# Weight sums of w_down made in DRAM ahead of the down projection, and its products in a new order

## The chip, the cores and the metric

The kernel runs on one core of a Trainium2 chip, and the other cores are idle. The metric is the device time of one execution in microseconds (us). Kernels are compared by the median of several executions; a comparison is called faster or slower from 2% on.

## What is computed

One layer of a bidirectional encoder, all in float32, on 512 tokens of width 1024 with 256 memory tokens:

```
n = rms_norm(x);  proj = n @ w_in                       # 1024 x 4608
ya = s5_branch(proj[:, :512])                           # state-space scan both ways, GLU
yb = sgu_branch(zu, zv)                                 # gated mixing in chunks of 128 tokens
h = x + (sigmoid(ga) * (ya @ w_proj_a) + sigmoid(gb) * (yb @ w_proj_b)) @ w_out
h = h + cross_attention(rms_norm(h), rms_norm(mem))     # w_q, w_k, w_v, w_xo; 4 heads
h = h + (silu(hn @ w_gate) * (hn @ w_up)) @ w_down      # w_down: 2816 x 1024
out = rms_norm(h)
```

The change concerns the last product, with w_down: 512 tokens by 2816 by 1024.

## The kernel before, in words

Every matrix product runs in a two-part float32r form: each operand is split into a high and a low part (`split`, lines 83 to 86: a cast on ScalarE and a subtraction on VectorE), and three TensorE matmuls, high by high, high by low and low by high, make one product (`mm3`). So each weight block is loaded, split, and used.

The stages follow each other: the norm of x and its transposition; half of `zv`; the S5 input; the other half of `zv`; the gates `ga`; `zu`; the gates `gb` with w_proj_b; the GLU and w_proj_a; w_out; w_k, w_v, w_q with the attention; w_xo; the gate and up units; the down projection. The S5 scan is a generator (`s5_program`) whose pieces are worked off beside the matmuls of the other mixers, by a credit that `tick` hands out.

**The weight plan.** All weight blocks stand in one list, `plan`, in the order of their use. Each entry has a key, a list of loads with a lead (how many blocks before its use the load is issued), and a function that makes the split operands. `next_w` (line 287) is called for each block: it calls `begin` for the entries up to FAR blocks ahead, which issues every load whose lead is due, and splits the blocks up to SPLITS = 2 ahead. An ordinary block is 512 KB, has a lead of LOADS = 3, lands in one of three `raw` buffers by a transfer on SyncE's queue (SP), and is split into one of three pairs of `hi` and `lo` buffers.

**The order on the engines.** The source issues through a tile framework with `schedule_with_timeline_sim=True`: at compile time a scheduler puts the instructions of each engine and queue in order, by the source's order and by when it expects their operands and buffers to be there, and it adds all semaphore waits. The position in the source is therefore not by itself the position in a queue. On the chip each engine and each queue then keeps its order. SP issues plain transfers, ScalarE's queue (ACT) a few more; GpSimd (POOL) issues transfers that add to their destination, and also computes the `pow` of the norms, clears the buffers `bd` and `ss` of the S5 part, adds in the merge and moves the S5 kernels through DRAM (`kd`, `tt`).

**Seven products.** The gate, up and down projections use a scheme with seven half-size products in place of eight: numbers 1 to 7, each of a sum of token quarters by a sum of weight quarters, with results added and subtracted. In the units (`plan_unit`) the weight sums are made by an adding transfer and by VectorE. In the down projection (`plan_down`, line 206) the quarter of w_down is 1408 by 512. It is cut into CHUNKS = 6 pieces (five of 2 x 128 rows, 512 KB, and one of 128 rows, 256 KB); one product is 66 matmuls with 512 columns, over two token tiles. Before the change the weight operands come like this:

- product 1: the first quarter, loaded into six tiles (`grown`) of the units' buffers, five blocks ahead;
- products 5, 6 and 4: the same tiles, after each use grown by another quarter with an adding transfer on POOL's queue (`grow`, line 222), which can start only when the split of that piece is done;
- products 2 and 3: plain loads into the `raw` buffers;
- product 7: a plain load into a large tile (`third_start`, line 231), and an adding transfer onto it (`third_add`, line 234), 16 and 14 blocks ahead.

The token operands are made by `make_tokens` (line 1326): for each product three pieces are split, and with products 5, 6 and 2 VectorE makes the next token sums in place. The results go onto `h` with `onto_h`; `first_half` and `finish` are the two halves of the last norm. The order of products is DOWN = 1, 5, 6, 2, 7, 3, 4, written out by hand a second time in the calls of `down_product` at the end.

Of the kernel before, what the change touches and what calls it, by code (L numbers as in the profile page):

```python
# [9 lines left out]
F32 = mybir.dt.float32  # L10
F32R = mybir.dt.float32r
AF = mybir.ActivationFunctionType
ALU = mybir.AluOpType
# [4 lines left out]
P = 128  # L18
D = 1024
T = 512  # L20
NT = T // P
KD = D // P
# [11 lines left out]
NF = FF // P  # L34
# [18 lines left out]
def hybrid_layer_kernel(  # L53
# [8 lines left out]
    nc = tc.nc  # L62
# [3 lines left out]
    w_gate, w_up, w_down = w_gate[0], w_up[0], w_down[0]  # L66

    cp = ctx.enter_context(tc.tile_pool(name="const", bufs=1))
    wp = ctx.enter_context(tc.tile_pool(name="weights", bufs=3))
    sp = ctx.enter_context(tc.tile_pool(name="slots", bufs=1))  # L70
    np_ = ctx.enter_context(tc.tile_pool(name="norm", bufs=2))
    dp = ctx.enter_context(tc.tile_pool(name="scratch", bufs=1, space=DRAM))
# [10 lines left out]
    def split(dst_hi, dst_lo, src, lo_eng=None):  # L83

        nc.scalar.copy(dst_hi, src)  # L85
        (lo_eng or nc.vector).tensor_tensor(dst_lo, src, dst_hi.bitcast(F32), ALU.subtract)  # L86
# [1 line left out]

    LOADS, SPLITS, FAR = 3, 2, 16
    plan, tiles = [], []

    def block(w, kb, k, c0, n):
        return w[kb * P:(kb + k) * P, c0:c0 + n].rearrange("(k p) c -> p k c", p=P)

    def halves(src, j=None, place=None):
        _, k, n = src.shape
        if place is None:
            hi = wp.tile([P, k, n], F32R, tag="hi", name="whi", bufs=3)  # L100
            lo = wp.tile([P, k, n], F32R, tag="lo", name="wlo", bufs=3)
        else:
            hl = sums_place(place, k, n)
            hi, lo = hl[:, 0], hl[:, 1]
        split(hi, lo, src, nc.gpsimd if j is not None and j < 2 else None)
        return hi, lo
# [3 lines left out]
    def sums_place(i, k, n, shift=0):  # L110
        t = sums_pool[0].tile([P, 2 * k * n + 128], F32R, tag=f"s{i}", name=f"s{i}", bufs=1)
        return t[:, shift:shift + 2 * k * n].rearrange("p (h k n) -> p h k n", h=2, k=k)
# [20 lines left out]
    def plan_feat(w, c0, nk, kpt=4):  # L133
        for kb in range(0, nk, kpt):
            plan_block(w, kb, kpt, c0, 256)

    def plan_tok(w, c0, nk, kpt=2):
        for kb in range(0, nk, kpt):
            plan_block(w, kb, kpt, c0, 512)
# [7 lines left out]
    stp = [None]  # L147
# [52 lines left out]

    DOWN, CHUNKS = (1, 5, 6, 2, 7, 3, 4), 6
    third = []

    def plan_down(w, make_tokens):
        def b(i, jc, c):
            row, k = (4 * c + 2 * i, 2) if c < CHUNKS - 1 else (NF - 2 + i, 1)
            return block(w, row, k, 512 * (1 - jc), 512)

        grown, got = {}, {}

        def view(t, c):
            return t if c < CHUNKS - 1 else t[:, 0:1]

        def first(c):
            nm = ("t", "b22", "b21")[c % 3]
            grown[c] = stp[0].tile([P, 2, 512], F32, tag=nm, name="grown", bufs=2)
            nc.sync.dma_start(view(grown[c], c), b(0, 0, c))

        def grow(c, src):
            nc.gpsimd.dma_start(view(grown[c], c), src, accum_op=ALU.add)

        def plain(q, c, src):
            got[q, c] = wp.tile([P, 2, 512], F32, tag="raw", name="wraw", bufs=3)
            nc.sync.dma_start(view(got[q, c], c), src)

        def third_start(c):
            if not third:
                third.append(token_place("t3", F32).rearrange("p (c k n) -> p c k n", c=8, k=2))  # L230
            nc.sync.dma_start(view(third[0][:, c], c), b(0, 1, c))

        def third_add(c):
            nc.gpsimd.dma_start(view(third[0][:, c], c), b(1, 1, c), accum_op=ALU.add)

        for q in DOWN:
            for c in range(CHUNKS):
                loads = {1: [(5, lambda c=c: first(c))],
                         2: [(LOADS, lambda c=c: plain(2, c, b(1, 0, c)))],
                         3: [(LOADS, lambda c=c: plain(3, c, b(1, 1, c)))],  # L240
                         7: [(16, lambda c=c: third_start(c)), (14, lambda c=c: third_add(c))]}.get(q, [])

                def make(q=q, c=c):
                    if c % 2 == 0:
                        make_tokens(q, c // 2)
                    src = got.pop((q, c)) if q in (2, 3) else third[0][:, c] if q == 7 else grown[c]
                    ops_ = halves(view(src, c))
                    if q in (1, 5, 6):
                        grow(c, b(*{1: (0, 1), 5: (1, 1), 6: (1, 0)}[q], c))
                    return ops_  # L250

                plan.append(((w, q, c), loads, make))

    plan_tok(w_in, OFF_V, KD)
    for c0 in range(0, SW, 256):
        plan_feat(w_in, c0, KD)
    plan_tok(w_in, OFF_V + 512, KD)
    for c0 in range(0, D, 256):
        plan_feat(w_in, OFF_GA + c0, KD)
    for c0 in range(0, GW, 256):  # L260
# [20 lines left out]
    UNITS = [(w, c0) for c0 in range(0, FS, 512) for w in (w_gate, w_up)]  # L281
    plan_units(UNITS)
    down_tokens = []
    plan_down(w_down, lambda q, c: down_tokens[0](q, c))
    used_w = [0]

# [192 lines left out]
    def slot(tag, shape, dt, name):  # L479
        return sp.tile(list(shape), dt, tag=tag, name=name)  # L480

    def token_place(name, dt, shift=0):
        t = sp.tile([P, 2 * KD * T + 128], dt, tag="B", name=name)
        return t[:, shift:shift + 2 * KD * T]

    def token_slot(name, shift=0):

        hl = token_place(name, F32R, shift).rearrange("p (h k t) -> p h k t", h=2, k=KD)
        return hl[:, 0], hl[:, 1]


# [557 lines left out]
    h = slot("A", (P, NT, D), F32, "h")  # L1049
# [45 lines left out]
    shift = ap_.tile([P, 16], F32, name="shift")  # L1095
# [87 lines left out]
    fn = (fn_hi, fn_lo)  # L1183
# [89 lines left out]
    def unit_bank(name):  # L1273
        return bank(name).rearrange("p (j t) -> p j t", j=2)
# [7 lines left out]
    def put(u, f, ts, src):  # L1282
        dst = acts(u[1] // 512, f)[:, :, ts]
        if u[0] is w_gate:
            nc.scalar.activation(dst, src, AF.Silu)
        else:
            nc.vector.tensor_tensor(dst, dst, src, ALU.mult)
# [38 lines left out]
    def make_tokens(q, c):  # L1326
        hl = sums_place((1, 2, 4)[len(made) % 3], 4, 256)
        made[q, c] = (hl[:, 0], hl[:, 1])
        f, ts = {1: (0, T0), 5: (0, T1), 6: (0, T1), 2: (1, T0), 7: (0, T0), 3: (1, T0), 4: (1, T1)}[q]
        for src, ks in token_pieces(f, ts, c):  # L1330
            split(hl[:, 0, ks], hl[:, 1, ks], src)
        a, b_, c_, d_ = (token_pieces(f_, ts_, c) for ts_ in (T0, T1) for f_ in (0, 1))
        for (q11, _), (q12, _), (s21, _), (q22, _) in zip(a, b_, c_, d_):
            if q == 5:
                V.tensor_tensor(s21, s21, q11, ALU.subtract)
            elif q == 6:
                V.scalar_tensor_tensor(q11, s21, -1.0, q22, ALU.mult, ALU.subtract)
            elif q == 2:
                V.tensor_tensor(q12, q12, s21, ALU.add)
# [3 lines left out]
    for i, u in enumerate(UNITS):  # L1343
        final = i == len(UNITS) - 1
        x, v = begun
        q = unit_bank("pq")
# [38 lines left out]
    def first_half(t, half):  # L1385

        early[t] = half
        sum_sq(hss[:, 2, t, half:half + 1], h[:, t, HALF[half]])
        nc.vector.tensor_tensor(hg[:, t, :], h[:, t, HALF[half]], g_o[:, HALF[half]], ALU.mult)
        nc.vector.tensor_scalar(msq[:, t:t + 1], hss[:, 2, t, half:half + 1], 1.0 / D, EPS, ALU.mult, ALU.add)  # L1390
# [8 lines left out]
    def finish(t):  # L1399
        half = 1 - early[t]  # L1400
        sum_sq(hss[:, 2, t, half:half + 1], h[:, t, HALF[half]])
        r = inv_root(t, hss[:, 2, t, half:half + 1])
        later(0.5, lambda: write(t, r))
# [33 lines left out]
    def down_product(ps, q, start):  # L1437
        for c in range(CHUNKS):
            rows_product(ps, q, c, next_w(w_down, q, c), (0, 1), slice(0, 512), start and c == 0, c == CHUNKS - 1)

    def onto_h(ps, t0, half, op):
        for t in range(2):
            hs = h[:, t0 + t, HALF[half]]
            nc.vector.tensor_tensor(hs, hs, ps[t], op)

    dx, dv = ([bank(nm + str(t)) for t in range(2)] for nm in ("dx", "dv"))
    dq = [bank("dq0"), aux("dq1")]
# [2 lines left out]
        nc.scalar.copy(dv[t], dx[t])  # L1450
    down_product(dq, 5, True)
    onto_h(dq, 2, 0, ALU.add)
    down_product(dx, 6, False)
    onto_h(dx, 0, 0, ALU.subtract)
    down_product(dv, 2, False)
    onto_h(dv, 0, 1, ALU.add)
    for t in range(2):
        first_half(t, 1)
    down_product(dx, 7, False)
    onto_h(dx, 2, 0, ALU.subtract)  # L1460
    for t in range(2, 4):
        first_half(t, 0)
    down_product(dq, 3, False)
    onto_h(dq, 0, 0, ALU.add)
    for t in range(2):
        finish(t)

    held = []
    for c in range(CHUNKS):
        ops_ = next_w(w_down, 4, c)  # L1470
# [9 lines left out]
    for i in range(2):  # L1480
        p = aux("pcut", (P, 256))
# [37 lines left out]
```

## Time and profile before

| | us |
|---|---|
| median of 3 runs | 929.71 |
| lowest and highest of them | 928.16 and 939.89 |
| the profiled execution, its own time | 929.5 |
| its span in the trace | 927.7 |
| mixers, attention, w_xo | 0 to about 590 |
| gate and up units | 590 to about 798 |
| down projection | about 798 to 920.7 |
| last norm's end and output | 920.7 to 927.7 |

The profile has one row for each engine: PE is TensorE's matmuls and PEld its weight loads, DVE is VectorE, ACT ScalarE, POOL GpSimd, SP the queue of SyncE; a name with q is the sequencer or queue of that engine. A row of a view by stretches has the stretch, its length, then busy time and number of instructions of PE, PEld, DVE, ACT and POOL, then the granted TensorE clock (1 is full), the busy share of the 16 DMA engines and the GB/s that they moved. A row of the chain that ended last has start, length and what ran or was waited for. A row of the timeline has start, length, engine, line, operation, destination and sources; a bracket behind it is the idle time before it and what ended that. A row of waits has who waited for whom, and us in total, number, and the longest. A row of a group ends in busy us and mean ns of one, and then idle time before it. DMA rows end in the size and the us from issue to landing.

### The profile page before, as it was taken

The numbers are of one execution on the slowest core, as the hardware profiler recorded it, in microseconds if no ns is written. First come the engines' busy times: TensorE is split into PE (matmuls) and PEld (weight loads), VectorE is DVE, ScalarE is ACT, GpSimd is POOL, SyncE is SP. The second block draws the span as 40 slices with busy tenths as digits, with TensorE's granted clock in tenths as the row PEclk, the third lists the DMA queues.
The fourth block names the chain that finished last, engine by engine and source line by source line (L and its number), as shares of the span: only waits on it lengthen the run. The fifth ranks groups of instructions, "written<-read, shape, count | busy, mean of one in ns | idle before, by whom it ended". The sixth has DMA issues, their size and how long they took to land.

```text
span 927.7 us, 14071 instructions
## 1 busy us (share of the span) xinstructions
PE 902.2 (97%) x5510; PEld 791.2 (85%) x5510; DVE 608.3 (66%) x991; ACT 458.6 (49%) x671; POOL 114.2 (12%) x163
## 2 busy tenths in 40 slices
PE   7999999999999999999999999999999999879996
PEld 6788888888888888789898888999999999757785
DVE  5596562989653247658535535777876778748875
ACT  5443995144464244436425434745555555435564
POOL 3004210000034103300000001001000000244001
PEclk9999999999999999999999999999999999989999
DMA  8445223333233363634531219225545553799612
GB/s 270 124 129 141 77 93 102 125 103 102 91 105 88 102 195 121 218 114 159 182 114 68 70 62 256 69 91 144 131 130 144 146 141 113 223 207 206 180 58 90
DMA packets 99298, 122.58 MB, mean 132 GB/s; under 512 B 12560, under 2 KB 72480, under 8 KB 99232
## 3 DMA queue, kind: packets, MB, share of 16 engines
q1 hardware_dynamic: 82720, 99.95, 33.5%
q0 software_dynamic: 13344, 19.37, 11.7%
q10 hardware_dynamic: 3168, 2.36, 0.9%
q8 instruction: 43, 0.70, 0.3%
q14 instruction: 23, 0.19, 0.1%
HBM read 114.88 MB, written 6.78 MB: 131 GB/s over the span
## 4 chain that ended last, share of the span: by engine, by line
PE 79%; DMA 8%; ACT 5%; DVE 4%; issue 2%; POOL 1%; POOLq 0%; SPq 0%; ACTq 0%; DVEq 0%
PE pf L315 31%; PE pt L315 12%; PE px L1268 12%; PE pq L1268 6%; DMA grown<-in_w_down_dram 3%; PE dx L315 3%; PE pv L1268 3%; PE dq L315 2%; PE pk L718 1%; DVE wlo L86 1%; ACT whi L85 1%; DMA wraw<-in_w_up_dram 1%; PE po L315 1%; PE psc L315 1%; PE ptr L467 1%
## 5 line engine op out<-in xcount | busy, mean ns | idle before, releaser
L86 DVE TENSOR_TENSOR wlo<-wraw,whi 128x1024 fp32r<-128x1024 f32 x100 | 123.7, 1238 | 124.2 <-ACT whi L85 116.6
L85 ACT CAST whi<-wraw 128x1024 fp32r<-128x1024 f32 x102 | 106.2, 1043 | 149.3 <-PE pf L315 80.3
L315 PE MATMUL pf<-xn,whi 128*128 128x512 f32 x448 | 140.9, 393 | 0.0
L315 PEld LDWEIGHTS pf<-xn,whi 128*128 128x128 f32 x448 | 83.7, 188 | 17.2 <-issue 0.2
L315 PE MATMUL pf<-xn,wlo 128*128 128x512 f32 x224 | 87.5, 391 | 0.0
L1268 PE MATMUL px<-fn,whi 128*128 128x256 f32 x480 | 83.9, 277 | 1.6 <-ACT u L1353 1.6
L1268 PEld LDWEIGHTS px<-fn,whi 128*128 128x128 f32 x480 | 72.5, 188 | 1.9 <-ACT u L1353 1.7
L85 ACT CAST whi<-b 128x1024 fp32r<-128x1024 f32 x40 | 42.2, 1054 | 54.5 <-PE px L1268 26.1
L86 DVE TENSOR_TENSOR wlo<-b,whi 128x1024 fp32r<-128x1024 f32 x40 | 48.9, 1224 | 28.0 <-ACT whi L85 27.9
L1268 PE MATMUL px<-fn,wlo 128*128 128x256 f32 x240 | 66.3, 276 | 0.0
L1268 PE MATMUL pq<-s,whi 128*128 128x256 f32 x320 | 55.1, 276 | 0.0
L85 ACT CAST whi<-t 128x1024 fp32r<-128x1024 f32 (+1 forms) x36 | 37.5, 1041 | 34.8 <-PE pv L1268 11.3
L315 PE MATMUL dx<-whi,s 128*128 128x512 f32 x170 | 53.3, 390 | 1.0 <-ACT whi L85 1.0
L86 DVE TENSOR_TENSOR wlo<-t,whi 128x1024 fp32r<-128x1024 f32 (+1 forms) x36 | 43.4, 1209 | 16.3 <-ACT whi L85 16.3
L315 PEld LDWEIGHTS pf<-xn,wlo 128*128 128x128 f32 x224 | 42.1, 188 | 8.5
L1268 PEld LDWEIGHTS pq<-s,whi 128*128 128x128 f32 x320 | 48.3, 188 | 0.2
L315 PE MATMUL pt<-whi,xn 128*128 128x512 f32 x128 | 43.2, 410 | 2.0 <-ACT xn L85 1.7
L1268 PEld LDWEIGHTS px<-fn,wlo 128*128 128x128 f32 x240 | 45.1, 188 | 0.0
L1268 PE MATMUL pq<-s,wlo 128*128 128x256 f32 x160 | 44.2, 276 | 0.0
L85 ACT CAST whi<-grown 128x1024 fp32r<-128x1024 f32 (+1 forms) x24 | 23.5, 978 | 38.8 <-DMA grown<-in_w_down_dram 23.0
L315 PE MATMUL pf<-hn,whi 128*128 128x512 f32 (+1 forms) x160 | 41.9, 349 | 0.0
L86 DVE TENSOR_TENSOR wlo<-grown,whi 128x1024 fp32r<-128x1024 f32 (+1 forms) x24 | 27.1, 1134 | 21.7 <-ACT whi L85 21.4
(381 smaller groups left out, 2256.3 us busy)
## 6 DMA issues: line engine op xcount, KB each, us to landing
wraw<-in_w_in_dram SPq DMA_DIRECT2D x36, 512.0 KB, 3.6
b<-in_w_gate_dram SPq DMA_DIRECT2D x15, 512.0 KB, 3.6
b<-in_w_up_dram SPq DMA_DIRECT2D x15, 512.0 KB, 3.6
grown<-in_w_down_dram POOLq DMA_DIRECT2D x15, 512.0 KB, 12.5
wraw<-in_w_down_dram SPq DMA_DIRECT2D x10, 512.0 KB, 3.7
wraw<-in_w_proj_b_dram SPq DMA_DIRECT2D x8, 512.0 KB, 3.3
wraw<-in_w_out_dram SPq DMA_DIRECT2D x8, 512.0 KB, 4.0
wraw<-in_w_k_dram SPq DMA_DIRECT2D x8, 512.0 KB, 4.4
```

Of the source, the lines that this page charges most:

```text
L85: nc.scalar.copy(dst_hi, src)
L86: (lo_eng or nc.vector).tensor_tensor(dst_lo, src, dst_hi.bitcast(F32), ALU.subtract)
L315: nc.tensor.matmul(ps, a[x], b[y], start=start and i == 0, stop=stop and i == 2, skip_group_check=free)
L467: nc.tensor.transpose(ps[:, j, :], src[:, k * P:(k + 1) * P], ident)
L718: nc.tensor.matmul(ps[32 * j:32 * j + 32, q, :], bd[i][:, g].rearrange("p d c -> p (d c)"), lc(es[i], g), start=(i == 0), stop=False, tile ...
L1268: nc.tensor.matmul(ps[:, j, :], a[x], b[y], start=start and j == k == i == 0, stop=k == 3 and i == 2, skip_group_check=True)
```

## The change

Four sums of quarters of w_down, one for each of the products 4, 5, 6 and 7, get places of their own in DRAM (`dsum`). They are made by 24 copies DRAM to DRAM on SP's queue and 24 adding transfers DRAM to DRAM on POOL's queue: `dsum` 5 and 7 start as a copy of one quarter and get another quarter added; 6 and 4 start as a copy and get the finished `dsum` 5 and 6 added. In the source the copies hang on the plan from the entry `first_copy` on, the first block of the gates `ga` (entry 12), one for each block; the adding transfers from 26 entries later, one for every second block, which reaches into w_xo. All of the down projection's operands are then plain loads into the `raw` buffers, three blocks ahead. The order of products becomes 1, 5, 2, 6, 3, 7, 4, and one token sum moves from product 6 to product 3. FAR, how far `next_w` looks ahead for due loads, becomes 7.

```diff
-    LOADS, SPLITS, FAR = 3, 2, 16
+    LOADS, SPLITS, FAR = 3, 2, 7
...
-    DOWN, CHUNKS = (1, 5, 6, 2, 7, 3, 4), 6
+    DOWN, CHUNKS = (1, 5, 2, 6, 3, 7, 4), 6
+    DSRC = {1: (0, 0), 2: (1, 0), 3: (1, 1)}
+    dsum = {q: dp.tile([P, NF // 2, 512], F32, name=f"dsum{q}") for q in (4, 5, 6, 7)}
+
+    def down_block(i, jc, c):
+        row, k = (4 * c + 2 * i, 2) if c < CHUNKS - 1 else (NF - 2 + i, 1)
+        return block(w_down, row, k, 512 * (1 - jc), 512)
+
+    def down_sum(q, c):
+        return dsum[q][:, 2 * c:min(2 * c + 2, NF // 2), :]
+
+    def plan_sums(first, adds):
+
+        def put(j, fn):
+            plan[j][1].append((0, fn))
+
+        for n, (q, i, jc) in enumerate(((5, 0, 0), (7, 0, 1), (6, 1, 1), (4, 1, 0))):
+            for c in range(CHUNKS):
+                put(first + 6 * n + c, lambda q=q, i=i, jc=jc, c=c:
+                    nc.sync.dma_start(down_sum(q, c), down_block(i, jc, c)))
+        more = {5: lambda c: down_block(0, 1, c), 7: lambda c: down_block(1, 1, c),
+                6: lambda c: down_sum(5, c), 4: lambda c: down_sum(6, c)}
+        for n, q in enumerate((5, 7, 6, 4)):
+            for c in range(CHUNKS):
+                put(adds + 2 * (6 * n + c), lambda q=q, c=c:
+                    nc.gpsimd.dma_start(down_sum(q, c), more[q](c), accum_op=ALU.add))
...
+                def load(q=q, c=c, got=got):
+                    src = down_block(*DSRC[q], c) if q in DSRC else down_sum(q, c)
+                    got["raw"] = wp.tile([P, 2, 512], F32, tag="raw", name="wraw", bufs=3)[:, :src.shape[1]]
+                    nc.sync.dma_start(got["raw"], src)
...
+                plan.append(((w, q, c), [(LOADS, load)], make))
...
+    first_copy = len(plan)
     for c0 in range(0, D, 256):
         plan_feat(w_in, OFF_GA + c0, KD)
...
+    plan_sums(first_copy, first_copy + 26)
     plan_down(w_down, lambda q, c: down_tokens[0](q, c))
...
-            elif q == 6:
+            elif q == 3:
                 V.scalar_tensor_tensor(q11, s21, -1.0, q22, ALU.mult, ALU.subtract)
...
     down_product(dq, 5, True)
     onto_h(dq, 2, 0, ALU.add)
-    down_product(dx, 6, False)
-    onto_h(dx, 0, 0, ALU.subtract)
     down_product(dv, 2, False)
     onto_h(dv, 0, 1, ALU.add)
     for t in range(2):
         first_half(t, 1)
+    down_product(dx, 6, False)
+    onto_h(dx, 0, 0, ALU.subtract)
+    down_product(dq, 3, False)
+    onto_h(dq, 0, 0, ALU.add)
+    for t in range(2):
+        finish(t)
     down_product(dx, 7, False)
     onto_h(dx, 2, 0, ALU.subtract)
     for t in range(2, 4):
         first_half(t, 0)
-    down_product(dq, 3, False)
-    onto_h(dq, 0, 0, ALU.add)
-    for t in range(2):
-        finish(t)
```

The functions `first`, `grow`, `plain`, `third_start` and `third_add` of `plan_down` go, and with them the large tile `t3`.

More of the change, by code (lines that the diff above doesn't have):

```diff
@@ L197, in plan_units @@
             plan.extend(e for e in (m[5], m[6], nx.get(1), m[7], nx.get(2), m[4], m[3]) if e is not None)
-    DOWN, CHUNKS = (1, 5, 6, 2, 7, 3, 4), 6
-    third = []
-    def plan_down(w, make_tokens):
[L207 to L234, printed above, removed]
@@ L236, in plan_down, with make @@
+    def plan_down(w, make_tokens):
         for q in DOWN:
             for c in range(CHUNKS):
[L238 to L243, printed above, removed]
+                got = {}
+                def load(q=q, c=c, got=got):
+                    src = down_block(*DSRC[q], c) if q in DSRC else down_sum(q, c)
+                    got["raw"] = wp.tile([P, 2, 512], F32, tag="raw", name="wraw", bufs=3)[:, :src.shape[1]]
+                    nc.sync.dma_start(got["raw"], src)
+                def make(q=q, c=c, got=got):
@@ L244, in make @@
                     if c % 2 == 0:
                         make_tokens(q, c // 2)
[L246 to L252, printed above, removed]
+                    return halves(got.pop("raw"))
+                plan.append(((w, q, c), [(LOADS, load)], make))
@@ L480, in slot @@
         return sp.tile(list(shape), dt, tag=tag, name=name)
-    def token_place(name, dt, shift=0):
-        t = sp.tile([P, 2 * KD * T + 128], dt, tag="B", name=name)
-        return t[:, shift:shift + 2 * KD * T]
     def token_slot(name, shift=0):
-        hl = token_place(name, F32R, shift).rearrange("p (h k t) -> p h k t", h=2, k=KD)
+        t = sp.tile([P, 2 * KD * T + 128], F32R, tag="B", name=name)
+        hl = t[:, shift:shift + 2 * KD * T].rearrange("p (h k t) -> p h k t", h=2, k=KD)
         return hl[:, 0], hl[:, 1]
```

## The prediction, made before the result was known

> **What bounds the kernel now.** I read the page's head first, then busy time by stretches, then the chain that ended last, then TensorE's timeline around the breaks in that chain.
>
> ```profile
> span 927.7 us, 14071 instructions
> PE 902.2 (97%) x5510; PEld 791.2 (85%) x5510; DVE 608.3 (66%) x991; ACT 458.6 (49%) x671; POOL 114.2 (12%) x163
> GB/s 270 124 129 141 77 93 102 125 103 102 91 105 88 102 195 121 218 114 159 182 114 68 70 62 256 69 91 144 131 130 144 146 141 113 223 207 206 180 58 90
> ```
>
> ```profile
> 45.00:93.00 48.00, 48.00 (x327) 39.68 (x326) 38.34 (x53) 18.00 (x37) 9.55 (x20) 1.00 0.47 134
> 590.00:786.00 196.00, 196.00 (x1679) 194.01 (x1678) 151.69 (x151) 104.82 (x128) 10.27 (x8) 1.00 0.47 124
> 786.00:798.60 12.60, 10.03 (x82) 9.44 (x81) 8.70 (x9) 6.02 (x7) 1.20 (x1) 1.00 0.47 147
> 798.60:920.70 122.10, 113.88 (x495) 91.66 (x493) 89.21 (x108) 63.10 (x84) 28.60 (x25) 0.96 0.72 162
> 816.00:834.00 18.00, 11.71 (x37) 7.89 (x35) 6.25 (x8) 4.60 (x7) 6.67 (x7) 0.81 1.13 206
> 834.00:854.00 20.00, 19.05 (x76) 15.29 (x77) 14.98 (x17) 11.50 (x14) 8.39 (x8) 0.91 1.13 206
> 920.70:927.70 7.00, 0.00 (x0) 0.00 (x0) 2.25 (x6) 2.49 (x8) 1.57 (x2) 0.82 0.39 150
> ```
>
> TensorE bounds the kernel: it is busy without a gap through the mixers and the gate and up units. The exception is the down projection, 798.6 to 920.7. There the DMA engines are over-full (share 1.13 at 206 GB/s), TensorE waits, and the granted clock falls to 0.81. Chain and timeline give the size:
>
> ```profile
> 814.34 18.88 DMA grown<-in_w_down_dram
> 839.93 11.12 DMA grown<-in_w_down_dram
> 861.50 7.74 DMA wraw<-in_w_down_dram
> 875.66 14.96 PE dx L315 x66
> 890.62 14.96 PE dq L315 x66
> ```
>
> ```profile
> 815.97 0.39 PE L315 MATMUL dq<-whi,s 128*128 128x512 f32 x1
> 843.77 0.61 PE L315 MATMUL dx<-whi,s 128*128 128x512 f32 x2
> 858.73 0.61 PE L315 MATMUL dv<-whi,s 128*128 128x512 f32 x2
> 875.50 0.62 PE L315 MATMUL dx<-whi,s 128*128 128x512 f32 x2
> ```
>
> An undisturbed product takes 14.96 us: 66 matmuls at 0.227. Product 5 (dq) lasts from 815.97 to 843.77, 27.8 us, so 12.8 are lost; its cause is the adding transfers into `grown`. Product 2 (dv) takes 16.8, 1.8 lost. All that waiting for `w_down` costs is 14.6 us, 1.6% of the profiled execution's 929.5 us (the median of the runs is 929.71, the same for this purpose). 2% would be 18.6 us, about what a measurement of this kernel can tell from no change. So even a perfect down stage, with the 2.6 us of 786 to 798.6 beside it, saves 17.2 us and does not reach it.
>
> **The change part by part.**
>
> *The down stage: -14.6.* The 24 adding transfers leave it. Every operand is a plain load of 512 KB, one per 12 matmuls or 2.72 us, three blocks ahead. The trace has the same pace elsewhere:
>
> ```profile
> 444.06 21.79 PE pt L315 x96
> ```
>
> ```profile
> wraw<-in_w_v_dram SPq DMA_DIRECT2D x8, 512.0 KB, 3.5
> ```
>
> Those are eight blocks of w_v, 2.72 us each, without a break, landing in 3.5 us. So 42 loads at that pace cost nothing; TensorE covers them. If a load took over some 6 us (three buffers of 2.72, less the split of 2.3 below), each chunk would be late by the excess.
>
> *VectorE in the new order: +1.6.*
>
> ```profile
> L86 DVE TENSOR_TENSOR wlo<-wraw,whi 128x1024 fp32r<-128x1024 f32 x100 | 123.7, 1238 | 124.2 <-ACT whi L85 116.6
> L85 ACT CAST whi<-wraw 128x1024 fp32r<-128x1024 f32 x102 | 106.2, 1043 | 149.3 <-PE pf L315 80.3
> ```
>
> ```profile
> L86 DVE TENSOR_TENSOR s<-a_up,s 128x1024 fp32r<-128x1024 f32 x6 | 7.3, 1220 | 0.0
> L1444 DVE TENSOR_TENSOR h<-h,dq 128x512 f32<-128x512 f32 x4 | 2.7, 684 | 0.2 <-PE dq L315 0.2
> L1335 DVE TENSOR_TENSOR a_up<-a_up 128x1024 f32<-128x1024 f32 x2 | 2.4, 1222 | 0.0
> ```
>
> A product needs 5.5 x 1.24 for weights, 2.75 x 1.22 for tokens and 2 x 0.68 for `h`, 11.6 us; where token sums are made (products 5, 2 and 3) 2.75 x 1.22 more, 15.0 us against 14.96. It just fits, and the neighbours have room. Bounds 0 and 3 x 1 us; I take 1.6.
>
> *Order of products, FAR: 0.* 2 before 6 and 3 before 7 respect the token sums. `finish` of tokens 0 and 1 moves ahead of product 7, under TensorE. The 7.0 us behind the last matmul stay. FAR 7 still covers the longest lead left, 7.
>
> *Copies and adding transfers: where the risk is.* Four quarters of 11 blocks of 256 KB are 11.5 MB: 24 copies on SP's queue, and 24 adding transfers on POOL's. The source hands the copies out one per weight block from the first gate block on, the adding ones one per two blocks from the 26th. But a copy reads an input and writes fresh DRAM, so it waits for nothing, and the trace shows what happens to such transfers:
>
> ```profile
> 16.47 0.43 SPq L919 DMA_DIRECT2D wsx<-in_sgu_w_dram  x1
> 17.52 0.83 SPq L922 DMA_DIRECT2D gbr<-in_sgu_ln_b_dram  x1
> 18.45 2.76 SPq L124 DMA_DIRECT2D wraw<-in_w_in_dram  x2
> 34.26 0.34 SPq L557 DMA_DIRECT2D rowbi<-in_s_b_im_dram  x1
> 34.70 0.38 SPq L124 DMA_DIRECT2D wraw<-in_w_in_dram  x1
> ```
>
> ```profile
> 150.22 0.33 SPq L425 DMA_DIRECT2D g_mem<-in_mem_norm_g_dram  x1
> ```
>
> ```profile
> 45.64 5.89 PE pf L315 x26
> ```
>
> Lines 919 and 922 stand in the source directly ahead of the first copy, behind twelve weight blocks, and went out at 16.5 and 17.5 us. `g_mem` belongs behind the mixers and went out at 150. So I expect the copies from 18 us on, wherever SP has a gap, and the adding ones as copies land, on POOL, which is 12% busy. "Beside the mixers" becomes "beside the first 150 us".
>
> How many transfers can stand ahead of a load:
>
> ```profile
> 1.67 1.14 ACTq L505 DMA_DIRECT2D xt<-in_x_dram  x2
> 2.17 0.60 SPq L124 DMA_DIRECT2D wraw<-in_w_in_dram  x1
> 4.51 0.33 SPq L504 DMA_DIRECT2D xt<-in_x_dram  x1
> ```
>
> ```profile
> SPq L504 <- DMA xt<-in_x_dram: 1.7, 1, 1.7
> ```
>
> ```profile
> 554.14 0.37 SPq L124 DMA_DIRECT2D wraw<-in_w_gate_dram  x1
> ```
>
> ```profile
> 563.93 11.69 DMA wraw<-in_w_up_dram
> ```
>
> These are the third and fourth issue on ACT's queue, the fourth and the fifth on SP's: with eight transfers out, SP holds a load that needs nothing until an earlier one lands. Of ten loads that go out from 554.1 on, the tenth, at 563.9, takes 11.7 us. So a weight load finds up to eight transfers ahead. At 206 GB/s (the adding stretch, the nearest row with extra traffic) one takes 2.54 us and eight 20.4; at the 270 GB/s of the page's first slice, 15.5. The room: weight block 6 is issued at 34.7, and its matmuls come two blocks of 24 x 0.227 = 5.4 us behind 45.64, at 56.5; less the split (1.04 + 1.24) 19.5 us. So copies alone are just hidden. With adding transfers taking every second turn, eight take up to 40.8. Issue to use spans five blocks less two splits, so a block then takes (40.8 + 4.6) / 5 = 9.1 us instead of 5.4, 3.6 lost, over the 10 blocks or so that pass meanwhile: 36 us. Bounds 0 and 36. Adding transfers follow the copies and overlap about half of them, so no row speaks for an end, and I take the middle, +18.
>
> The Trainium skill ("DMA: Bandwidth & Descriptors", section "Latency and other measured facts") gives 207 to 214 GB/s for copies between HBM tensors. By its 214 the copies would take an estimated 54 us; the trace has no such copy. The same page, "Queues, rings and completion order", says that an engine takes each ring in order and changes between rings packet by packet; by that rule, which speaks against the change, a weight load stands behind the copies of its own queue, and the 11.7 us row agrees.
>
> Also moved are POOL's 24 issues, off the down stage:
>
> ```profile
> 806.27 1.20 POOL L234 DMA_DIRECT2D t<-in_w_down_dram  x1 [8.42 <-DMA t<-in_w_down_dram]
> ```
>
> At 1.2 us each they are 29 us of POOL's time. Each waits for its copy, and POOL runs in order; behind it stand the `pow` of the norms, the clearing of `bd` and the S5 stores. SP's copies stand ahead of the S5 parameter rows (34.26 above) too.
>
> **The sum.** 929.5 - 14.6 + 1.6 + 18 = 934.5.
>
> **The rivals.**
>
> *All of it hidden: 916.5.* The copies drop into gaps between loads, or stay where the source puts them; 929.5 - 14.6 + 1.6. For it: 45 to 93 has a DMA share of 0.47, so half of 48 us is free there, and 19.5 us of room against 20.4. Against: copies and adding transfers at 206 GB/s are 112 us of all DMA engines.
>
> *One run of copies: slower, 955.* SP has nothing else between 21 and 34 us, so most copies go out there in one run ahead of weight block 6. That block then lands at 18.4 + 56 + 3.5 = 77.9 and is split by 80.2, not 56.5: 24 us of idle TensorE. After idle time the clock drops: product 5 lost 12.8 us where the chain of stretches 816 to 854 shows 6.3 + 1.0 us idle, a factor of 1.77, so 24 to 42 us. Middle 33, and POOL's `pow` and `bd` held behind unlanded copies some 5.5: 929.5 - 13 + 38.5 = 955. It decides for slower from 31.6 us of loss at the start (948.1). For it: `wsx` and the 10 us gap on SP. Against: a load that becomes ready goes ahead of copies not yet issued.
>
> *Faster by over 2%, under 911:* would need the 17.2 us whole and something that no row shows.
>
> **How the numbers follow.** Forecast (922 to 948) 0.36, hidden (911 to 922) 0.27, one run (over 948) 0.33, faster 0.04. The likeliest's own range is 922 to 948. For 8 in 10 the range goes from 913, where the hidden case has kept most of its gain, to 962, where the long run has cost 45 us. Faster 0.04, within 2% 0.63, slower 0.33.
>
> **What would show it.** Right: in 798.6 to 920.7 seven products of 15 to 15.5 us, DMA share near 0.5, clock 1.0. Copies to `dsum` on SP before 40 us; weight loads between 18 and 120 us that land in 15 to 40 us instead of 3.6; TensorE short by 10 to 30 us before 150. Wrong: copies issued at 90 to 240 us, or TensorE still gapless before 150 (then 916); a gap of over 30 us before block 6, or POOL waiting for `dsum` ahead of `r` or `bd` (then 950 and more); VectorE the wait of products 5, 2 and 3; or S5 results late at the GLU, which has no spare time now.

## The result and the profile after

The changed kernel takes 1004.22 us (median of 6 runs, 1000.4 to 1013.91) against 930.07 us for the kernel before (6 runs, 926.46 to 939.89): a ratio of 1.0798, 95% interval 1.0727 to 1.087. It is slower by 8%, beyond the predicted range of 913 to 962. The profiled execution took 1001.46 us, and its span is 72.0 us longer than before.

The head of the page after, with the lines that answer to those of before:

```profile
span 999.7 us, 14158 instructions
PE 903.6 (90%) x5510; PEld 792.5 (79%) x5510; DVE 610.5 (61%) x991; ACT 458.4 (46%) x671; POOL 107.7 (11%) x163
PE   7910279999999999799999999999999999999996
PEclk9965589999999999899999999999999999999999
GB/s 277 257 240 253 249 160 146 118 101 85 85 104 86 106 85 107 159 84 218 138 147 190 85 85 43 178 158 41 151 128 146 134 135 147 48 121 184 203 225 105
```

TensorE's work is what it was (903.6 us against 902.2). The time is one hole: a slice is 25 us long, and from the third to the fifth TensorE is all but idle, its granted clock falls to 0.5, and the DMA engines move about 250 GB/s, twice what they moved there before. The stretches of the kernel after:

```profile
18.00:45.00 27.00, 27.00 (x127) 21.82 (x126) 14.03 (x42) 11.95 (x24) 7.34 (x7) 0.94 1.01 262
45.00:93.00 48.00, 9.16 (x41) 7.26 (x39) 6.17 (x31) 4.00 (x11) 9.00 (x9) 0.64 1.06 245
93.00:140.00 47.00, 21.22 (x104) 17.26 (x104) 8.44 (x9) 6.36 (x11) 7.34 (x9) 0.68 0.95 237
883.00:993.00 110.00, 108.36 (x497) 89.68 (x495) 90.03 (x113) 64.27 (x90) 2.56 (x3) 1.00 0.57 178
```

From 45 to 93, where the kernel before had 48.00 busy of 48, TensorE has 9.16. The last row is the down projection: full clock, a DMA share of 0.57 in place of 0.72, hardly a gap. What SP issued in those slices (start, length, count):

```profile
18.75 4.66 SPq L222 DMA_DIRECT2D dsum<-in_w_down_dram  x5
...
30.25 55.62 SPq L222 DMA_DIRECT2D dsum<-in_w_down_dram  x13
85.96 5.76 SPq L549 DMA_DIRECT2D rowbi<-in_s_b_im_dram  x1
92.79 1.20 SPq L124 DMA_DIRECT2D wraw<-in_w_in_dram  x1
```

This is the whole story in four lines. The S5 parameter row `rowbi` and weight block 6 went out at 34.26 and 34.70 before; now 21 copies stand ahead of them (the 5, three more behind a weight block at 23.5, and the 13), and they go out at 85.96 and 92.79. The 13 copies hold SP for 55.62 us, 4.28 each. TensorE's waits, from 0 to 200 us and from 300 to 440:

```profile
PE pbc L558 <- DMA rowbi<-in_s_b_im_dram: 58.6, 1, 58.6
PE pf L310 <- ACT whi L85: 5.6, 1, 5.6
```

```profile
PE pf L310 <- ACT yg_hi L85: 7.4, 1, 7.4
```

TensorE works in order and stands at the transposition of `rowbi`; when that comes, block 6 is hardly later. The third wait is the GLU: the S5 branch, started late, is late there too. The chain after, and one row of the chain before, show where the 72 us arise:

```profile
92.79 26.39 DMA wraw<-in_w_in_dram
...
246.12 5.19 PE psv L958 x46
...
528.23 21.79 PE pt L310 x96
...
883.43 1.39 PE dx L310 x6
...
900.83 14.96 PE dq L310 x66
915.79 14.96 PE dv L310 x66
...
990.49 1.32 PE pcut L310 x11
```

```profile
173.58 3.63 PE psv L966 x32
```

The mixers' spatial products end at 177.2 before and 251.3 after: 74.1 lost. At the w_v stage (444.06 before, 528.23 after) it is 84.2, so the GLU and what follows add some 10. The first product of the down projection starts 84.8 later. Then that stage takes 991.8 - 883.4 = 108.4 us in place of 122.1: 13.7 won back. The end behind it takes 7.9 in place of 7.0. 84.8 - 13.7 + 0.9 = 72.0.

### The profile page after: what moved, and what is told of

It reads as the page before. It is cut to its first block, busy times and chain, and to the rows that moved or that the text cites. A ratio compares the mean times of both kernels' runs of the same rounds, so it can differ in the third digit from the quotient of the medians.

```text
span 999.7 us, 14158 instructions
## 1 busy us (share of the span) xinstructions
PE 903.6 (90%) x5510; PEld 792.5 (79%) x5510; DVE 610.5 (61%) x991; ACT 458.4 (46%) x671; POOL 107.7 (11%) x163
## 2 busy tenths in 40 slices
DMA packets 105987, 142.77 MB, mean 143 GB/s; under 512 B 13232, under 2 KB 73152, under 8 KB 105920
## 3 DMA queue, kind: packets, MB, share of 16 engines
q1 hardware_dynamic: 90688, 120.14, 38.9%
q0 software_dynamic: 12064, 19.37, 11.1%
## 4 chain that ended last, share of the span: by engine, by line
PE 80%; DMA 9%; DVE 4%; SPq 3%; ACT 2%; issue 1%; POOL 0%; ACTq 0%; POOLq 0%; DVEq 0%
PE pf L310 30%; PE px L1260 11%; PE pt L310 10%; PE dx L310 6%; PE pq L1260 5%; DMA wraw<-in_w_in_dram 4%; DMA dsum<-in_w_down_dram 3%; PE dq L310 3%; SPq L222 3%; PE pv L1260 3%; PE dv L310 1%; PE pk L710 1%; PE pz L767 1%; DVE wlo L86 1%; DMA b<-in_w_gate_dram 1%
## 5 line engine op out<-in xcount | busy, mean ns | idle before, releaser
L86 DVE TENSOR_TENSOR wlo<-wraw,whi 128x1024 fp32r<-128x1024 f32 (+1 forms) x130 | 157.7, 1216 | 121.1 <-ACT whi L85 119.7
L85 ACT CAST whi<-wraw 128x1024 fp32r<-128x1024 f32 x132 | 135.2, 1028 | 171.1 <-PE pf L310 68.6
L558 PE MATMUL pbc<-ident,rowbi 32*128 32x32 f32 x16 | 2.0, 294 | 58.6 <-DMA rowbi<-in_s_b_im_dram 58.6
L86 DVE TENSOR_TENSOR wlo<-t,whi 128x1024 fp32r<-128x1024 f32 x30 | 36.7, 1224 | 16.3 <-ACT whi L85 16.3
L85 ACT CAST whi<-t 128x1024 fp32r<-128x1024 f32 x30 | 31.6, 1053 | 31.8 <-PE pv L1260 11.3
```

Source lines behind the costliest of these rows:

```text
L558: nc.tensor.transpose(ps[:, c, :], rows[:, :, c], ident[:G, :G])
```

## The experiments

Two theories stood against each other. *Queue order*: the copies wait for nothing, so the compile-time order put them in one run ahead of the rows and of block 6, and TensorE stands behind that run. *Traffic*: the 23 MB of the sums cost TensorE wherever they lie. (11.54 MB are copied and 11.53 added; the kernel before adds as many, so the page's total grows by 20 MB, from 122.58 to 142.77.) Neither came through whole. Losses below are counted from 918, the time with the copies spread out. Kernels without a number of runs ran once; the kernel before, run once beside each of two groups of them, took 937.43 and 935.31 us. The third column is when TensorE starts the units in the trace (the row of 96 matmuls `pf` in each chain; 680.73 in the changed kernel, 596.03 before). It leaves out a difference of 7 us inside the units, which comes up below.

| kernel | us | units start | what it says |
|---|---|---|---|
| one copy per weight block | 918.08 (4 runs) | 594.22 | all of the loss gone |
| one copy per two blocks | 922.08 (10 runs) | 599.77 | the same within the spread of the times |
| no sums at all | 921.22 (4 runs) | 593.92 | the floor is no lower |
| rows on another queue | 1011.31 | 683.70 | block 6 is late as well |
| 12 copies free | 950.05 | 629.17 | 32 lost |
| 6 copies free | 915.66 | 594.75 | nothing lost |
| no adding transfers | 944.86 | 617.42 | 27 lost |
| copies on POOL's queue | 962.98 | 642.60 | 45 lost past SP's order |
| the run later | 989.52 | 668.52 | 71 lost elsewhere too |
| adding transfers in one run, later | 951.0 | 630.46 | 33 lost without any copy ahead |
| no sums, old order of products | 920.23 | 594.19 | the order wins nothing |

**Spread out, or left out.** The copies keep their bytes and their number, but each is tied on SP behind the weight block loaded last before it in the source:

```diff
-                nc.sync.dma_start(got["raw"], ...)
+                last_load[:] = [nc.sync.dma_start(got["raw"], ...).ins]
...
-                    nc.sync.dma_start(down_sum(q, c), down_block(i, jc, c))
+                    with tc.issue_after(last_load[0]):
+                        nc.sync.dma_start(down_sum(q, c), down_block(i, jc, c))
```

> Each copy is tied behind the weight block loaded last before it in the source, so the 24 copies alternate with weight blocks on SP's queue instead of going out in one run; bytes, copies and adding transfers are the same. Theory of the queue's order (the loss came from a run of 21 copies issued ahead of the S5 row rowbi and of weight block 6): rowbi is issued at about 34 us again instead of 86, TensorE is without a break of over 5 us before 150, and the time is the before's 930.1 less the 13 of the down stage, 917, with 916 to 922 as the range. Theory of the traffic (23 MB more through the DMA engines cost TensorE wherever they lie): weight blocks land in over 10 us throughout the mixers, the granted clock falls there, and the time stays at 940 or more.

With `first + 2 * (6 * n + c)`, one per two blocks:

> As the kernel with one copy per weight block, but one copy per two blocks, so that the copies reach from about 60 us to over 300. Theory of the queue's order: 915 to 920, within 2 us of the kernel with one per block, since either leaves the rows and the weight blocks in time. Theory of the traffic: a gain over one per block of half of what that one loses, and still 935 or more.

Without the call of `plan_sums`, and with `DSRC.get(q, (0, 0))` for the operands, so that products 4 to 7 read a plain quarter in place of a sum:

> Leaves out the weight sums: no copies and no adding transfers, all seven products load a quarter of w_down as it is. It is the floor of the change: what the down stage gives when the sums cost nothing. Both theories: 930.1 less 13, 915 to 918, the seven products 14.96 us each; whatever the two kernels with held copies take above it is the cost of the traffic.

One per block: 918.08 us, ratio to before 0.9874 (0.9837 to 0.9912). One per two blocks: 922.08, 0.991 (0.9867 to 0.9953). The floor: 921.22, 0.9888 (0.9836 to 0.9941). By their times the three can't be told apart, so what spread transfers cost lies within the spread of the runs; the second and third medians lie a few us above what was expected of them. Against the kernel before, all three count as the same by the 2% of this text, though their intervals lie below 1. SP and the landing of the weight blocks from 80 to 300 us, with one copy per block:

```profile
34.05 0.34 SPq L553 DMA_DIRECT2D rowbi<-in_s_b_im_dram  x1
...
80.58 0.39 SPq L125 DMA_DIRECT2D wraw<-in_w_in_dram  x1
81.03 0.62 SPq L222 DMA_DIRECT2D dsum<-in_w_down_dram  x1
91.11 0.37 SPq L125 DMA_DIRECT2D wraw<-in_w_in_dram  x1
```

```profile
45.00:93.00 48.00, 48.00 (x327) 39.67 (x326) 38.42 (x51) 17.67 (x35) 10.64 (x21) 1.00 0.56 150
200.00:300.00 100.00, 100.00 (x586) 84.39 (x584) 62.96 (x176) 49.53 (x58) 25.96 (x52) 1.00 0.73 193
```

```profile
DMA to landing us min/median/max: 3.4/4.4/10.4
```

`rowbi` is in time, copies and blocks take turns, the DMA share rises to 0.73 beside the mixers, and TensorE stays at 48.00 of 48 and 100.00 of 100. Blocks land in 4.4 us at the median.

One reading of the spread belongs here. The profiled execution of this kernel has a span of 920.0, that of the floor 912.0; both reach the units at the same time (chain of the one, then of the other):

```profile
594.22 16.64 PE pf L314 x96
...
803.83 1.38 PE dx L314 x6
```

```profile
593.92 16.65 PE pf L309 x96
...
796.63 1.39 PE dx L309 x6
```

So up to there the copies and adding transfers cost 0.3 us. One copy per two blocks is not as free: it reaches the units at 599.77, 5.5 us later. Its last copies go out at 409 us, and from 360 to 420 the DMA share is 0.81 and TensorE is busy for 57.22 us of 60, against 59.43 with one per block. The units, which the change does not touch, take 209.6 us in one execution and 202.7 in the other, at a granted clock of 1.00 in both. Of the 13 profiled executions, one for each kernel, four have the longer units. Whether that goes with the execution or with the kernel is not shown, though the floor's own four runs, 913.83 to 923.72, differ by as much. A single time is therefore read to about 7 us, and stages are compared instead.

**Which of the two that stand behind the run.** Only the rows go past the copies:

```diff
-                nc.sync.dma_start(row, ...)
+                (nc.sync if nm == "br" else nc.scalar).dma_start(row, ...)
...
-                    nc.sync.dma_start(row[:, :, d, :], src[0, d])
+                    nc.scalar.dma_start(row[:, :, d, :], src[0, d])
```

> As the changed kernel, but the S5 parameter rows (rowbi, rowcr, rowci) are issued on the queue of ACT, past the run of copies on SP; the weight blocks stay behind the run. If the rows alone made the loss: no wait for rowbi, about 940. If rows and weight block 6 both stand behind the run, the second is late anyway: TensorE waits for the weight split of block 6 (issued at about 86 to 93 us) instead of rowbi, and the time is 985 to 1000. Theory of the traffic: 995 to 1004, with a wait spread over many blocks.

1011.31 us. SP's run and TensorE's longest wait:

```profile
30.48 58.09 SPq L222 DMA_DIRECT2D dsum<-in_w_down_dram  x14
```

```profile
PE pf L310 <- ACT whi L85: 66.0, 2, 37.6
```

The wait for `rowbi` is gone and 66.0 us of waiting for weight splits stand in its place. Rows alone are not the cause; both stand behind the run. The time is above what was expected because a second block waits again (37.6 of the 66.0 is the first), and 7 us more are the units once more (209.6). At the start of the units the two kernels are within 3.0 us of each other (683.70 and 680.73), so sending the rows past the run gains nothing.

**How many copies.** Twelve of the copies stay free, those of the first two sums; or six, with `q == 5`. The rest are tied:

```diff
+            if q in (5, 7):
+                nc.sync.dma_start(down_sum(q, c), down_block(i, jc, c))
+            else:
+                with tc.issue_after(last_load[0]):
+                    nc.sync.dma_start(down_sum(q, c), down_block(i, jc, c))
```

> As the changed kernel, but only the first two sums' copies (12 of 24) are free to go early; the last 12 are tied behind weight blocks as in the kernel with one copy per block. Queue order: some 4 of the 12 still stand behind the eight that go out at once, and each of these costs SP the 4.3 us that one of the 13 copies of the run took, so rowbi is issued at about 45 to 50 us and weight block 6 at 50 to 55; the block lands about 20 us behind, 72 to 77, against a use at 56.5, so TensorE stands for 15 to 25 us instead of 64, and the time is 940 to 955: the loss goes with the number of copies ahead of the block. If a loss came from the adding transfers or the traffic as a whole, which are the same here, it would stay above 980.

> As the kernel with 12 copies free to go early, but with six (the first sum); the other 18 are tied behind weight blocks. With 12 free the loss against the kernel with none free was about 32 us, with 24 it was 83. If the loss goes with the run of copies past the eight that can be out at once, six cost nothing: rowbi at 34 us, 917 to 925. If every transfer in the first 100 us costs its share of the DMA engines, six copies and their six adding transfers cost a quarter of 83 to 45 us: 929 to 939.

950.05 and 915.66 us, both as the theory of the queue's order had it (the second 1.3 us below its range). SP and TensorE with twelve:

```profile
29.59 16.34 SPq L222 DMA_DIRECT2D dsum<-in_w_down_dram  x4
46.02 1.89 SPq L556 DMA_DIRECT2D rowbi<-in_s_b_im_dram  x1
```

```profile
PE pbc L565 <- DMA rowbi<-in_s_b_im_dram: 17.9, 1, 17.9
```

Eight of them go out by 27 us; the four past them hold SP for 16.34 us, 4.1 each. With six:

```profile
18.00:45.00 27.00, 27.00 (x129) 21.86 (x128) 16.19 (x51) 13.62 (x27) 7.31 (x7) 0.96 1.03 270
45.00:93.00 48.00, 48.00 (x302) 39.30 (x301) 38.16 (x57) 17.97 (x33) 4.61 (x10) 1.00 0.69 187
```

SP holds no copy, and TensorE is busy for 48.00 us from 45 to 93 though the DMA share from 18 to 45 is 1.03. So a full set of DMA engines for some 25 us is covered by the blocks already loaded.

**The copies without the adding transfers.** The loop over `more` is left out.

> Leaves out the 24 adding transfers, so the four sums hold only their first quarter; the 24 copies go out early as in the changed kernel. It tells how much of the run's length is the copies' own and how much the adding transfers beside them. If the adding transfers take half of the DMA engines' time: the 21 copies are through by about 65 to 72 us instead of 86, TensorE's wait shrinks by 15 to 20 us, and the time is 965 to 980. If the copies alone hold SP as long, 995 to 1004. If the loss were the adding transfers' alone, 917 to 925.

```profile
30.93 20.01 SPq L222 DMA_DIRECT2D dsum<-in_w_down_dram  x13
51.71 0.35 SPq L542 DMA_DIRECT2D rowbi<-in_s_b_im_dram  x1
```

944.86 us, between the cases foreseen and in none of them: the adding transfers take more of the run than the half assumed, and the copies alone are not free. The same 13 copies take 20.01 us, 1.54 each, not 55.62. The adding transfers, each released as its copy lands, nearly triple the run, and 57 of the 83 us lost go with them. (At the start of the units, 63 of 86; this execution has the longer units.)

**Past SP's queue.** All copies on POOL's queue, tied behind the last `pow` of x's norm:

```diff
+            with tc.issue_after(last_pow[0]):
+                nc.gpsimd.dma_start(down_sum(q, c), down_block(i, jc, c))
```

> All 24 copies are issued on the queue of POOL instead of SP's, tied behind the last pow of x's norm; the adding transfers stay there too. SP's queue has only loads, so rows and weight blocks wait for no copy, but they share the DMA engines with as many copies and adding transfers at the same time as in the changed kernel. Theory of the queue's order: rowbi at about 34 us, weight blocks land in 4 to 10 us, time 917 to 928. Theory of the traffic: loads land in over 19 us from 30 to 110, TensorE stands at many blocks, 950 or more.

962.98 us: here the theory of the queue's order fell in its simple form. SP issues in time, but the blocks do not land (SP, then the landing of the 14 blocks issued from 34 to 154 us, then ScalarE's wait):

```profile
34.07 0.34 SPq L553 DMA_DIRECT2D rowbi<-in_s_b_im_dram  x1
```

```profile
DMA to landing us min/median/max: 3.5/25.0/35.1
```

```profile
ACT whi L85 <- DMA wraw<-in_w_in_dram: 56.6, 13, 15.9
```

A 512 KB block beside a standing run on another queue takes 25.0 us at the median where it takes 3.6 alone. By an estimate, three buffers then give one block per 25.0 / 3 = 8.3 us. The Trainium skill ("DMA: Bandwidth & Descriptors", section "Issuing engines are not separate DMA queues") says that transfers issued from several engines run on the same 16 DMA engines and that another issuer saves only issue time. The 45 us that remain agree. The 38 that went (1001.5 to 963.0) are time on SP's queue, but far from small: the 13 copies held it for 55.62 us. Not all of the 45 us are late blocks: POOL's own work for S5 now stands behind the copies (the clearing of `bd` starts at 122.17 us, before at 77.80), and TensorE waits 7.2 us at the GLU.

**Elsewhere.** Is it the start that is special? All 24 copies tied behind the block of entry 24 (`put(first + 12, ...)`), and, in another kernel, the copies spread but all adding transfers in one run behind the norm's last `pow` at 426 us, long after the last copy (issued at 245). The edit of the second, in part:

```diff
+    with tc.issue_after(last_pow[0]):
+        for add in late_adds:
+            add()
     for c0 in range(0, D, 256):
         feat(w_k, c0, mn, KD, k_evac, n=M)
```

> All 24 copies still go out in one run on SP, but behind the weight block of entry 24 (about 160 to 200 us) instead of at 18 us; the adding transfers follow as they land. If the loss is that of the run, wherever it lies, the weight blocks behind it land some 65 us late and the time is 980 to 1005. If it is special to the start (the S5 rows, the first blocks), 918 to 940.

> Copies tied one per weight block as in the kernel that does so, but all 24 adding transfers released in one run behind the last pow of the norm at about 424 us, when all copies have landed and POOL has nothing else until 560. No copy stands on SP's queue then. The adding transfers need about 71 us of all DMA engines (the share of the software queue, 12.6% of 920 less 4.9% of 912), and 60% of the 137 us is free. If only the sum of the demand counts, they fit: 917 to 923. If a weight load beside a standing run of adding transfers gets less than it needs (25 us to landing, as in the kernel with the copies on POOL's queue, so 8.3 us per block with three buffers instead of 2.7 to 5.4), TensorE stands for 25 to 50 us between 424 and 520 and the time is 943 to 970.

989.52 and 951.0 us. SP and TensorE with the later run of copies:

```profile
185.09 70.37 SPq L222 DMA_DIRECT2D dsum<-in_w_down_dram  x24
255.56 20.36 SPq L125 DMA_DIRECT2D wraw<-in_w_in_dram  x3
```

```profile
PE pf L314 <- ACT whi L85: 70.5, 2, 69.8
```

The same hole at another place: 70.37 us of run, 69.8 of waiting, no S5 row in it. With the run of adding transfers: the stretch, the same stretch of the kernel with six copies free, and the landing of weight blocks from 424 to 515 us:

```profile
420.00:520.00 100.00, 77.30 (x437) 64.86 (x436) 36.44 (x47) 28.13 (x40) 23.61 (x25) 0.90 0.95 221
```

```profile
420.00:520.00 100.00, 99.84 (x618) 89.58 (x617) 56.75 (x91) 45.75 (x81) 0.55 (x1) 1.00 0.37 123
```

```profile
DMA to landing us min/median/max: 3.4/10.5/27.2
```

No copy is on SP's queue, and the demand would fit by its sum: from the queues' shares of the spans (one copy per block, then the floor) the copies take 0.404 x 920.0 - 0.369 x 912.0 = 35 us of all 16 engines and the adding transfers 0.126 x 920.0 - 0.049 x 912.0 = 71 us, and with a share of 0.37 some 60% of 137 us is free. Yet TensorE stands for 22.7 of 100 us, and its clock is 0.90. The shares, of the one and then the other:

```profile
q1 hardware_dynamic: 90688, 120.14, 40.4%
q0 software_dynamic: 12064, 19.37, 12.6%
```

```profile
q1 hardware_dynamic: 87232, 108.60, 36.9%
q0 software_dynamic: 7328, 7.84, 4.9%
```

**The order of products alone.** No sums, and the seven products in the order of before:

> As the floor (no weight sums, all loads plain), but with the order of products of the kernel before: 1, 5, 6, 2, 7, 3, 4. Leaves out the weight sums. If the new order is worth nothing of its own, the seven products take 15.0 us each here too and the time is within run to run differences of the floor, 913 to 924; if VectorE's token sums in products 5 and 2 next to one another bound the old order, a product is 1 to 3 us longer and the stage that much.

920.23 us. The chain of this kernel, and the end of that of the floor:

```profile
803.80 1.39 PE dx L309 x6
...
909.80 1.32 PE pcut L309 x11
```

```profile
903.35 1.32 PE pcut L309 x11
```

From the first product's start to the last matmul's end the old order takes 107.3 us, the new one (from 796.63) 108.0. The new order wins nothing and costs 0.7.

## Why the prediction was wrong

*The down stage: right.* Foreseen were -14.6 and +1.6, so -13.0; measured is -13.7. The products in the middle take 14.96 us. The 1.6 for VectorE in the new order was somewhat high: the two kernels without sums differ by 0.7, and in the changed kernel the last product takes 16.2 us (975.6 to 991.8), where it took 15.1 before.

*Where the transfers go: right.* The copies went out from 18.75 and the adding ones as they landed, not beside the attention. That SP holds with eight out fits the runs too: of twelve free copies it let eight go and was held by the next four, POOL's queue issued eight copies and then waited, and six copies cost nothing. Whether the limit of eight lies in the chip or in the waits that the framework adds is not shown. Tied behind weight blocks, the change takes 918.08 us, near the 916.5 of the hidden case: the bytes did fit.

*The term that failed is the start: +18, bounds 0 and 36.* It measured 84.8 (74.1 in the mixers, the rest at the GLU and behind it). Two steps of its working failed.

First, the forecast put at most eight transfers ahead of a load and argued that "a load that becomes ready goes ahead of copies not yet issued". SP's order is fixed when the kernel is built, and all 21 copies stood ahead. Block 6 did then find a queue of the foreseen size, its 26.39 us to landing lie between the 15.5 and the 40.8 of the prediction, but it joined that queue 58 us late. The one-run rival had this mechanism and should have been the forecast: the rows of SP that the prediction quotes leave it free from 21 to 34 us. (The trace has one more issue there, `mix` at 23.30, of 0.35 us; it changes nothing.)

Second, the rival's size. It priced the run at 22 transfers of 2.54 us, 56 us, with the adding transfers left out, and came to 24 us of idle TensorE. The runs show 1.54 us per copy without adding transfers and 4.28 with them. By rows of after: the run ends at 85.96, and block 6 is issued at 92.79, lands at 119.2 and is first used at 120.36. TensorE has stood still since 54.2, but for 2 us of transposing `rowbi`: its two waits are 58.6 + 5.6 = 64.2 us. Of the 9.9 us more up to the mixers' end, 6.8 are three later waits (1.6, 3.6 and 1.6 us); the rest goes with a granted clock of 0.92 from 120 to 182, where it was 1.00 before. The prediction's own sum of 112 us of all DMA engines was near the 35 + 71 measured; it was used against the hidden case and not put into the run.

*S5 late at the GLU* stood in the list of signs, without a price: 7.4 us. *POOL's `pow` and `bd`*, 5.5 in the rival, are not seen as a wait of TensorE.

What stays open: how the 45 us lost of the kernel with the copies on POOL's queue split between copies and adding transfers, and how the engines share between two queues. The Trainium skill (same page, "Queues, rings and completion order") has each engine take turns between queues by packets; no run here shows the turns, only that a block got 25 us.

## What to carry to other kernels

Bytes that fit in free DMA time still cost what they delay. Before hanging background transfers on a source position, ask what holds them there: one that waits for nothing goes early, in one run, and a load behind it in its queue, or beside it in another, is late by most of that run. Tie each one behind a transfer that the kernel already paces; here this turns 1.080 into 0.987 with the same bytes. That is no more than the gain of the down stage, 1.3%, and still below the 2% from which a kernel counts as faster.

## What was not expected of the hardware

- Copies DRAM to DRAM are fast: 11.54 MB (120.14 less 108.60) in 35 us of all engines is 328 GB/s. Without adding transfers the engines moved 323 GB/s, loads included, from 31 to 51 us at a share of 1.00. The Trainium skill ("DMA: Bandwidth & Descriptors", section "Latency and other measured facts") has 207 to 214 GB/s for tiles of another shape; here the measurement decides.
- Adding transfers DRAM to DRAM cost twice that: 11.53 MB (19.37 less 7.84) in 71 us, 162 GB/s. Both rates are by the packets' time, with the transfers spread out.
- The units ran 202.7 us in nine of the profiled executions and 209.6 in four, at the same granted clock of 1.00; why is open.
